# Quarter products for a second gate and up product, from the fourth pair of feature blocks on

## The chip, the core and the metric

The kernel runs on one core of a Trainium2 chip. The core has five engines with a queue each: TensorE (PE; its weight loads are PEld), VectorE (DVE), ScalarE (ACT), GpSimd (POOL) and SyncE (SP, which here only issues DMAs). An engine takes its instructions in the order of its queue and waits at semaphores. The metric is the time of one execution on the device in microseconds, the median of the runs shown.

## What is computed

One layer of an encoder block on 1024 tokens of width 1024, in float32: attention with forget gates and a pooling mixer, an output projection, and a SwiGLU. The change lies in the SwiGLU's first half, the gate and up products with 2816 features each:

```python
h2 = rmsnorm(x, norm2_g[layer])
gate = jnp.einsum('bsd,df->bsf', h2, w_gate[layer])
up = jnp.einsum('bsd,df->bsf', h2, w_up[layer])
x = x + jnp.einsum('bsf,fd->bsd', jax.nn.silu(gate) * up, w_down[layer])
```

## The kernel before

**Precision.** Every operand of a matmul is split into a high half, rounded by ACT, and a low half, the rest, taken by DVE (`split`, L119). A product is three matmuls, high by high, high by low and low by high (`mm3`, L159, so lines L161 to L163 in the profile).

**The stage.** The 22 feature blocks of 128 are taken in eleven pairs (j = 0 to 10). A pair is a 2 x 2 block product in Strassen's form with seven products instead of eight, P1, P2, P6, P7, P5, P3 and P4. The activations are the moving side, as blocks `b11`, `b21`, `t2`, `t3`, `t1`, `b22` and `t4` (high and low, L992) that are made once. The weights are the stationary side: per pair, raw tile 0 holds a11 and a12, raw tile 1 holds a21 and a22 (`gu_raw`, L1040, loaded by SP), and POOL makes four sums s1 to s4 from them (`gu_sums`, L1078): s1 = a21 + a22 for P5, s2 = s1 - a11 for P6, s3 = a11 - a21 for P7, s4 = a12 - s2 for P3. P1 takes a11, P2 a12, P4 a22. The second raw tile of the next pair can be loaded when P4's page has read the present one.

**Pages.** The split weights of one product are a page (`gu_page`, L999): ACT makes its high half, DVE its low half. There are three places for pages, so the page of a product can be made once the product three before it is done. `next_page` (L1358) makes the page two steps ahead, and issues the loads of the raw tiles and POOL's sums for the next pair.

**Products.** `product` (L1020) is 24 matmuls of 512 columns, 12 for the gate bank and 12 for the up bank. P1, P6, P5 and P3 share the banks c1 and go on adding in them; ACT takes a copy in between (`snap`, L1144) as sP1, sU2 and sU4. P2 has the banks c2; P7 and P4 share c3. From pair 1 on, P3 is itself done in Strassen's form, as seven quarter products Q1 to Q7 of six matmuls with 256 columns (`fine_product`, L1249): DVE makes sums of weight quarters in place (`fine_page`, L1224: one sum before page P3a, three before page P3b), and adds each quarter product's bank into the copy sU4. The quarters of P3 are laid among P4's matmuls, in an order written out (L1386). The quarters of the activation block b22 are made once, by `fine_steps` (L1181), during pair 1.

**Results.** The four corners of a pair are made in `after` (L1276): `corner` (L1158) adds a bank and a copy on DVE, takes Silu on ACT and multiplies on POOL. h11 comes from sP1 and P2, h22 from sU4 and P7, h21 from sU2 and P4, h12 from sU4 with P3 in it (Silu on ACT, product on DVE, L1289 and L1290). POOL makes four feature sums f1 to f4 (L1173), and ACT issues the spills of the features to DRAM (`spill`, L1268), from which the down stage reads them later.

**Order.** A pair's steps before are

```python
LATER = ("P1", "P2", "P6", "P7", "P5", "P3a", "P4", "P3b")
```

The order within each engine's queue is found by a planner from dependencies and the order of the program; `tc.issue_after(x)` puts what is issued under it behind x on x's engine.

Of the kernel before, what the change touches and what calls it, by code (L numbers as in the profile page):

```python
# [15 lines left out]
P = 128  # L16
# [29 lines left out]
def tile_kernel(  # L46
# [993 lines left out]
    def gu_raw(j, f, halves=(0, 1)):  # L1040

        if 0 in halves:
            raws[j, f] = xw_tile(f"r{f if j else 1 - f}", f"r{f}_{j}")
        f0 = (2 * j + f) * P
        cs = slice(halves[0] * 4, halves[-1] * 4 + 4)
        for n in range(2):
            dst = raws[j, f][:, n, :].rearrange("p (c e) -> p c e", e=P)
            nc.sync.dma_start(out=dst[:, cs, :], in_=wgu[n][:, cs, f0 : f0 + P])
# [24 lines left out]

    def gu_parts(j):
        r0, r1 = raws[j, 0], raws[j, 1]
        return r0[:, :, 0:512], r0[:, :, 512:1024], r1[:, :, 0:512], r1[:, :, 512:1024]

    def gu_sums(j):  # L1078
        a11, a12, a21, a22 = gu_parts(j)
        s1, s2, s3, s4 = (xw_tile(f"s{i}", f"s{i}_{j}", (P, 2, 512)) for i in (1, 2, 3, 4))  # L1080
        g = nc.gpsimd.tensor_tensor
        g(out=s1, in0=a21, in1=a22, op=ALU.add)  # L1082
        g(out=s2, in0=s1, in1=a11, op=ALU.subtract)
        g(out=s3, in0=a11, in1=a21, op=ALU.subtract)
        g(out=s4, in0=a12, in1=s2, op=ALU.subtract)
# [3 lines left out]
    s1, s2 = ([wk_tile("h", 8, f"s{i}_0{n}") for n in range(2)] for i in (1, 2))  # L1089
# [12 lines left out]
    def sum3():  # L1102
        s3 = operands[0]["P7"] = [wk_tile("h", 8, f"s3_0{n}") for n in range(2)]
# [4 lines left out]
    def sum4(n):  # L1108
        s4 = operands[0].setdefault("P3", [])
        s4.append(wk_tile("h", 8, f"s4_0{n}"))  # L1110
# [33 lines left out]
    def snap(j, key, n):  # L1144
        tag = ("h", 8) if key == "sU4" else ("su" if key == "sU2" else "sp", 2)
        t = snaps[j, key, n] = wk_tile(*tag, f"sn{j}_{key}{n}")
        nc.scalar.activation(out=t, in_=banks["c1", n], func=AF.Copy)
# [4 lines left out]
    def feature(j, name, key):  # L1152
        t = feats[name] = wk_tile("h", 8, f"{name}_{j}")
# [27 lines left out]
    def fine_steps(key):  # L1181
# [5 lines left out]
        t1 = const.tile([P, 2, 2, 256], R, tag="wmask", bufs=1, name=f"fine1_{key}")  # L1187
        fine[key, "Q5"] = t1[:, 0, :, :], t1[:, 1, :, :]

        def small(pl, tag, name):  # L1190
            return pl.tile([P, 2, 256], R, tag=tag, bufs=1, name=f"{name}_{key}")

        fine[key, "Q7"] = small(wk, "e2", "fine3h"), small(xw, "junk2", "fine3l")
        z = {}

        def whole(c, h):
            def do():
                at = ("h", 8) if c else (f"e{h}", 1)
# [10 lines left out]
        def parts(q, at):  # L1209
            def do():  # L1210
                if q == "Q6":
                    fine[key, q] = small(wk, "e0", "fine2h"), small(wk, "e1", "fine2l")
# [10 lines left out]

    def fine_page(j, k, part):  # L1224

        t = operands[j][k]
        p0, p1, p2, p3 = (t[:, n, h] for n in range(2) for h in QTR)

        def go(out, in0, in1, op):
            nc.vector.tensor_tensor(out=out, in0=in0, in1=in1, op=op)  # L1230

        if part == "a":
            go(p2, p0, p2, ALU.subtract)
            hi, lo = gu_page(f"gu{j}_{k}a", t)
            at = dict(Q1=0, Q2=1, Q7=2, Q4=3)
        else:
            go(p2, p3, p2, ALU.subtract)
            go(p1, p1, p2, ALU.subtract)
            go(p0, p0, p2, ALU.add)
# [9 lines left out]
    def fine_product(j, k, q, acc):  # L1249

        at = FINE_BANK[q]
        if q in ("Q1", "Q7", "Q2"):
            fine_banks[at] = bank(f"fine{at}_{j}{k}", *((BANKS["c2", 0], 1) if at == "C" else ("m", 2)))
# [14 lines left out]
    def spill(q=nc.scalar):  # L1268
        while spills:
            d, h = spills.pop(0)  # L1270
# [5 lines left out]
    def after(j, k):  # L1276
        if k in ("P1", "P6", "P5"):
            for n in range(2):
                snap(j, dict(P1="sP1", P6="sU2", P5="sU4")[k], n)
        if k == ("P2" if j else "P5"):  # L1280
            with tc.issue_after(at.ins) if j == 0 else ExitStack():
                corner(j, "h11", "sP1", "c2", "P1")
        if k == h22_from(j):
            corner(j, "h22", "sU4", "c3", "P4")
        if k == "P3":
            corner(j, "h12", None, "c1", None)
        if k == "P3b":
            acc = [snaps[j, "sU4", n] for n in range(2)]
            nc.scalar.activation(out=acc[0], in_=acc[0], func=AF.Silu)  # L1289
            nc.vector.tensor_tensor(out=acc[1], in0=acc[1], in1=acc[0], op=ALU.mult)  # L1290
# [16 lines left out]
    SUMS = dict(P5="b21h", P6="b21l", P7="t2h", P4="t2l")  # L1307
# [299 lines left out]
```

## Time and profile before

| | us |
|---|---|
| median of 3 runs (1032.22 to 1033.70) | 1032.89 |
| the profiled execution | 1032.35 |
| its span, first to last instruction | 1030.5 |
| gate and up stage | 395.60 to 813.60 |
| one pair in it | 37.78 |

The profile's page gives each engine's busy time and the chain of work that ended last, and further views answer single questions: busy time by stretches, the timeline (start, duration, engine, line, what is written from what, and in brackets how long the engine sat idle before it and who ended that), and the DMA issues. Starts are counted from the span's start. Tiles go by the program's names: `gu_P_l` is the low half of a page, `s` a sum of weights, `sn_sU` a copy, `fineA` a bank of quarter products, `r` a raw tile, `h` and `f` features, `hsdP` their place in DRAM.

### The profile page before, as it was taken

To read this page: it belongs to the slowest core of one execution; us is meant where nothing else is said; L and a number is where in the kernel's file an instruction comes from. 1 tells how busy PE (TensorE), PEld (TensorE's weight loads), DVE (VectorE), ACT (ScalarE), POOL (GpSimd) and SP (SyncE) were. 2 spreads that over 40 slices of the span, in tenths; PEclk is the share of its full clock that TensorE was granted. 3 is DMA by queue.
4 is the path that set the end of the run, shared out by engine and by line. 5 is a ranking of instruction groups with operands and counts; after the bars stand their busy time and mean duration, and the time that the engine had idled before them with its cause. 6 is when DMAs were issued, how large, how long until landed. Compare 5 with 4: busy or idle time off the path is not lost.

```text
span 1030.5 us, 14701 instructions
## 1 busy us (share of the span) xinstructions
PE 1021.7 (99%) x5284; PEld 874.5 (85%) x5284; DVE 716.0 (69%) x1132; ACT 464.9 (45%) x747; POOL 405.2 (39%) x315
## 2 busy tenths in 40 slices
PE   9999999999999999999999999999999999999997
PEld 8988888998988888888888888888888888888886
DVE  7565566776886579895556455556547899888886
ACT  7434355665675257533343333433333343333346
POOL 4350121214346043366548548557557410000045
PEclk9999999999999999999999999999999999999999
DMA  7214434333743133333243143233327574452424
GB/s 252 53 47 144 104 81 104 81 99 93 223 177 106 49 133 113 93 113 103 102 143 103 63 142 106 79 123 113 92 103 254 216 256 170 133 183 96 153 92 164
DMA packets 108249, 130.25 MB, mean 126 GB/s; under 512 B 7368, under 2 KB 70352, under 8 KB 108176
## 3 DMA queue, kind: packets, MB, share of 16 engines
q1 hardware_dynamic: 96544, 108.18, 33.2%
q10 hardware_dynamic: 11072, 19.69, 5.0%
q0 software_dynamic: 560, 1.44, 0.4%
q8 instruction: 42, 0.69, 0.3%
q14 instruction: 31, 0.25, 0.1%
HBM read 86.29 MB, written 33.03 MB: 116 GB/s over the span
## 4 chain that ended last, share of the span: by engine, by line
PE 98%; DMA 1%; POOL 0%; DVE 0%; issue 0%; ACT 0%; POOLq 0%; ACTq 0%
PE gu_P L162 12%; PE gu_P L161 12%; PE gu_P L163 12%; PE d L161 6%; PE d L162 6%; PE d L163 6%; PE po L657 4%; PE tp L643 3%; PE o L161 3%; PE qk L161 3%; PE qk L163 3%; PE qk L162 3%; PE o L162 3%; PE o L163 3%; PE v L374 2%; PE z L618 2%
## 5 line engine op out<-in xcount | busy, mean ns | idle before, releaser
L162 PE MATMUL d<-d,d 128*128 128x512 f32 (+1 forms) x308 | 118.6, 388 | 0.0
L163 PE MATMUL d<-d,d 128*128 128x512 f32 (+1 forms) x308 | 118.5, 388 | 0.0
L629 POOL TENSOR_SCALAR p<-p,rr 128x128 f32<-128x128 f32 (+3 forms) x64 | 48.5, 762 | 175.5 <-DVE rr L628 143.9
L161 PE MATMUL d<-d,d 128*128 128x512 f32 x308 | 107.8, 388 | 0.0
L120 ACT ACTIVATE d<-r_f 128x1536 fp32r<-128x1536 f32 (+1 forms) x28 | 38.7, 1384 | 107.6 <-PE d L162 107.6
L1169 POOL TENSOR_TENSOR h<-h,qh 128x512 f32<-128x512 f32 x33 | 64.0, 1941 | 34.5 <-ACT qh L1167 26.7
L1082 POOL TENSOR_TENSOR s<-r 128x1024 f32<-128x1024 f32 x10 | 24.0, 2401 | 131.0 <-DMA r<-in_w_up_dram 84.8
L121 DVE TENSOR_TENSOR gu_P_l<-r,gu_P_h 128x1024 fp32r<-128x1024 f32 x32 | 53.6, 1678 | 29.6 <-ACT gu_P_h L120 29.6
L120 ACT ACTIVATE gu_P_h<-r 128x1024 fp32r<-128x1024 f32 x32 | 33.8, 1059 | 86.2 <-issue 44.2
L1458 POOL TENSOR_SCALAR sse<-sse 128x1 f32<-128x1 f32 x7 | 3.5, 493 | 166.3 <-ACT junk L1454 166.1
L162 PEld LDWEIGHTS d<-d,d 128*128 128x128 f32 x308 | 57.8, 188 | 12.2 <-DVE d L121 0.2
L161 PEld LDWEIGHTS d<-d,d 128*128 128x128 f32 x308 | 57.8, 188 | 12.0
L163 PEld LDWEIGHTS d<-d,d 128*128 128x128 f32 x308 | 57.8, 188 | 11.8
L121 DVE TENSOR_TENSOR gu_P_l<-s,gu_P_h 128x1024 fp32r<-128x1024 f32 (+1 forms) x38 | 52.3, 1384 | 18.2 <-ACT gu_P_h L120 18.1
L626 ACT ACTIVATE p<-p,mn 128x128 f32<-128x128 f32 (+3 forms) x64 | 49.4, 772 | 32.2 <-DVE mn L620 29.3
L648 DVE TENSOR_TENSOR tl<-tp,th 128x512 fp32r<-128x512 f32 (+1 forms) x80 | 49.4, 632 | 9.6 <-ACT th L647 8.6
L121 DVE TENSOR_TENSOR d<-r_f,d 128x1536 fp32r<-128x1536 f32 (+1 forms) x28 | 47.6, 1702 | 6.5 <-ACT d L120 6.5
L163 PE MATMUL qk<-hTh,l_qk 128*128 128x512 f32 x128 | 50.7, 396 | 0.0
L161 PE MATMUL qk<-hTh,h_qk 128*128 128x512 f32 x128 | 50.6, 395 | 0.0
L162 PE MATMUL qk<-hTl,h_qk 128*128 128x512 f32 x128 | 50.4, 394 | 0.0
L647 ACT ACTIVATE th<-tp 128x512 fp32r<-128x512 f32 (+1 forms) x80 | 42.4, 550 | 15.2 <-PE tp L643 12.5
L1562 DVE TENSOR_TENSOR x2f_s<-d,x2f_s 128x512 f32<-128x512 f32 x64 | 42.3, 682 | 10.0 <-PE d L163 9.9
(802 smaller groups left out, 3218.5 us busy)
## 6 DMA issues: line engine op xcount, KB each, us to landing
r_f<-hsdP SPq DMA_DIRECT2D x77, 256.0 KB
r_wd<-in_w_down_dram SPq DMA_DIRECT2D x22, 512.0 KB
r<-in_w_gate_dram SPq DMA_DIRECT2D x21, 512.0 KB
r<-in_w_up_dram SPq DMA_DIRECT2D x21, 512.0 KB
hsdP<-f ACTq DMA_DIRECT2D x40, 256.0 KB
s<-hi SPq DMA_DIRECT2D x64, 128.0 KB
hsdP<-h ACTq DMA_DIRECT2D x32, 256.0 KB
x<-in_x_dram SPq DMA_DIRECT2D x8, 512.0 KB
```

What stands on the lines that cost most here:

```text
L120: mark["hi"] = nc.scalar.activation(out=hi, in_=src, func=AF.Copy)
L121: return eng.tensor_tensor(out=lo, in0=src, in1=f32(hi), op=ALU.subtract)
L161: nc.tensor.matmul(ps, lh, rh, start=start, stop=False, **kw)
L162: nc.tensor.matmul(ps, lh, rl, start=False, stop=False, **kw)
L163: mark["mm"] = nc.tensor.matmul(ps, ll, rh, start=False, stop=stop, **kw)
L626: nc.scalar.activation(out=pr[:, :n], in_=pr[:, :n], func=AF.Exp, scale=-1.0, bias=mn, accum_out=rs)
L629: nc.gpsimd.tensor_scalar(out=pr[:, :n], in0=pr[:, :n], scalar1=rr, scalar2=1.0, op0=ALU.mult, op1=ALU.mult)
L647: nc.scalar.activation(out=th[:, :w], in_=tp[:, :w], func=AF.Copy)
L648: nc.vector.tensor_tensor(out=tl[:, :w], in0=tp[:, :w], in1=f32(th[:, :w]), op=ALU.subtract)
L657: mark["pv"] = nc.tensor.matmul(po[:, first * P : 2 * P], vt[p][:, s, j, :], part[:, o : o + wd], start=(s == 0 and part is th), stop=(s = ...
L1169: nc.gpsimd.tensor_tensor(out=h, in0=h, in1=q, op=ALU.mult)
L1562: added = nc.vector.tensor_tensor(out=row, in0=ps, in1=row, op=ALU.add)
```

## The change

From pair 3 on (`BOTH = 3`), P2 too is done in seven quarter products, laid among P7's matmuls as P3's are among P4's. The block b21 gets quarters of its own, made during pair 2. The steps of such a pair are P1, P6, P2a, P7, P2b, P5, P3a, P4, P3b. The quarters of P2 are added into the copy sP1; h11 is then Silu of one half of it (ACT) times the other (POOL). Several things are put behind others: P7's page behind P2a's; P3a's page behind the addition of P2's last quarter; the three sums for P3b behind P3a's page, and P4's page behind these; POOL's four sums in the order s1 to s4; h12's multiplication behind the page of the next pair's P6. ACT issues the spills of these pairs three steps later. A raw tile is laid out by halves, gate and up next to each other, and loaded in four DMAs instead of two. There are 11 places for the small tiles instead of 8, and the room for them comes from the scratch space of DMA descriptors, set to 2 KB. For the last pair, sums of the down stage go to other tiles (`SUMS`).

```diff
-        for n in range(2):
-            dst = raws[j, f][:, n, :].rearrange("p (c e) -> p c e", e=P)
-            nc.sync.dma_start(out=dst[:, cs, :], in_=wgu[n][:, cs, f0 : f0 + P])
+        for a in halves:
+            to = raws[j, f][:, a, :].rearrange("p (n c e) -> p n c e", n=2, e=P)
+            for n in range(2):
+                nc.sync.dma_start(out=to[:, n, :, :], in_=wgu[n][:, 4 * a : 4 * a + 4, f0 : f0 + P])
...
+    RING = 11
+    BOTH = 3
...
-        g = nc.gpsimd.tensor_tensor
-        g(out=s1, in0=a21, in1=a22, op=ALU.add)
-        g(out=s2, in0=s1, in1=a11, op=ALU.subtract)
-        g(out=s3, in0=a11, in1=a21, op=ALU.subtract)
-        g(out=s4, in0=a12, in1=s2, op=ALU.subtract)
+        at = None
+        for out, in0, in1, op in (
+            (s1, a21, a22, ALU.add), (s2, s1, a11, ALU.subtract), (s3, a11, a21, ALU.subtract), (s4, a12, s2, ALU.subtract)
+        ):
+            with tc.issue_after(at.ins) if at and j >= BOTH else ExitStack():
+                at = nc.gpsimd.tensor_tensor(out=out, in0=in0, in1=in1, op=op)
...
+    def fine_sums(j, k, part):
+
+        p0, p1, p2, p3 = (operands[j][k][:, n, h] for n in range(2) for h in QTR)
+        later = ((p2, p3, p2, ALU.subtract), (p1, p1, p2, ALU.subtract), (p0, p0, p2, ALU.add))
+        for out, in0, in1, op in ((p2, p0, p2, ALU.subtract),) if part == "a" else later:
+            mark["sum"] = nc.vector.tensor_tensor(out=out, in0=in0, in1=in1, op=op)
+        summed.add((j, k, part))
...
         if k in ("P1", "P6", "P5"):
-            for n in range(2):
-                snap(j, dict(P1="sP1", P6="sU2", P5="sU4")[k], n)
-        if k == ("P2" if j else "P5"):
+            with tc.issue_after(mark["P3a"][1].ins) if k == "P5" and j >= BOTH else ExitStack():
+                for n in range(2):
+                    snap(j, dict(P1="sP1", P6="sU2", P5="sU4")[k], n)
+        if k == ("P2" if j else "P5") and j < BOTH:
...
+        if k == "P2b":
+            acc = [snaps[j, "sP1", n] for n in range(2)]
+            with tc.issue_after(mark["hi"].ins):
+                nc.scalar.activation(out=acc[0], in_=acc[0], func=AF.Silu)
+            nc.gpsimd.tensor_tensor(out=acc[1], in0=acc[1], in1=acc[0], op=ALU.mult)
...
-            nc.vector.tensor_tensor(out=acc[1], in0=acc[1], in1=acc[0], op=ALU.mult)
+            with tc.issue_after(mark["page"].ins):
+                nc.vector.tensor_tensor(out=acc[1], in0=acc[1], in1=acc[0], op=ALU.mult)
...
+    LAST = ("P1", "P6", "P2a", "P7", "P2b", "P5", "P3a", "P4", "P3b")
+    todo = [(j, k) for j in range(NG) for k in (LAST if j >= BOTH else LATER if j else FIRST)]
...
+    PIECES = (
+        ("Q1", "Q2", "Q7", (0, (0, 1)), (0, (2, 3)), "Q6", "Q4"), ((1, (0, 1)), "Q5", (1, (2, 3))), ("Q3",),
+    )
+    WINDOWS2 = {"P2a": (0, "P2", "P7"), "P7": (1, "P2", "P7"), "P2b": (2, "P2", "P7")}
+    WINDOWS3 = {"P3a": (0, "P3", "P4"), "P4": (1, "P3", "P4"), "P3b": (2, "P3", "P4")}
...
+        if i + 2 < len(todo) and k != "P2b":
+            with ExitStack() as order:
+                if k in ("P6", "P5") and j >= BOTH:
+                    for ins in (mark["page"], mark["hi"]):
+                        order.enter_context(tc.issue_after(ins.ins))
+                    if k == "P5":
+                        mark["P3a"] = mark["page"], mark["hi"]
+                        fine_sums(j, "P3", "b")
+                        order.enter_context(tc.issue_after(mark["sum"].ins))
+                next_page(*todo[i + 2])
+        waiting.append(spills[:])
+        spills.clear()
+        while len(waiting) > (1 if j < BOTH else 3):
             with tc.issue_after(mark["hi"].ins):
-                spill()
+                spill(waiting.pop(0))
...
+        if k == "P2b":
+            with tc.issue_after(mark["add"].ins):
+                next_page(*todo[i + 2])
...
+        if (j, k) == (BOTH - 1, "P1"):
+            q5, q7 = ([small(wk, f"g{n + m}", f"fine{n}{m}_b21") for m in range(2)] for n in (2, 4))
+            finer += fine_steps("b21", q5, q7, ("g0", "g1"))
...
-    nc = _bacc.Bacc("TRN2", target_bir_lowering=False, num_devices=1)
+    nc = _bacc.Bacc("TRN2", target_bir_lowering=False, num_devices=1, dynamic_dma_scratch_size=2048)
```

More of the change, by code (lines that the diff above doesn't have):

```diff
@@ L1179, in quarter, with small, fine_steps @@
         return t[:, 2 * c : 2 * c + 2, QTR[h]]
-    def fine_steps(key):
+    def small(pl, tag, name):
+        return pl.tile([P, 2, 256], R, tag=tag, bufs=1, name=name)
+    def fine_steps(key, q5, q7, ends):
         bh, bl = blocks[key]
@@ L1222, in fine_steps @@
         ]
+    summed = set()
+    def fine_sums(j, k, part):
[4 more added lines that the diff above has]
+        summed.add((j, k, part))
     def fine_page(j, k, part):
         t = operands[j][k]
-        p0, p1, p2, p3 = (t[:, n, h] for n in range(2) for h in QTR)
-        def go(out, in0, in1, op):
-            nc.vector.tensor_tensor(out=out, in0=in0, in1=in1, op=op)
+        if (j, k, part) not in summed:
+            fine_sums(j, k, part)
         if part == "a":
-            go(p2, p0, p2, ALU.subtract)
             hi, lo = gu_page(f"gu{j}_{k}a", t)
@@ L1266, in fine_product, with spill @@
             mark["add"] = nc.vector.tensor_tensor(out=out, in0=ps, in1=out, op=ALU.add)
-    def spill(q=nc.scalar):
-        while spills:
-            d, h = spills.pop(0)
+    def spill(due, q=nc.scalar):
+        for d, h in due:
             q.dma_start(out=d, in_=h)
```

74 lines of the change are left out of this document (33 added, 41 removed).

## The prediction

> **What bounds the kernel now.** I read the page first: the busy times, then the chain of work that ended last, by engine.
>
> ```profile
> PE 1021.7 (99%) x5284; PEld 874.5 (85%) x5284; DVE 716.0 (69%) x1132; ACT 464.9 (45%) x747; POOL 405.2 (39%) x315
> ...
> PE 98%; DMA 1%; POOL 0%; DVE 0%; issue 0%; ACT 0%; POOLq 0%; ACTq 0%
> ```
>
> TensorE is the chain. The change lies in the gate and up stage, so the next view is busy time by stretches: the whole stage, then one pair of feature blocks in it (pair 4, from the first matmul of its P1 to that of pair 5's).
>
> ```profile
> 395.60:813.60 418.00, 418.00 (x2047) 353.70 (x2046) 265.13 (x321) 163.90 (x223) 240.09 (x116) 1.00 0.35 116
> ...
> 548.36:586.14 37.78, 37.78 (x187) 32.06 (x186) 21.92 (x28) 13.91 (x18) 23.60 (x12) 1.00 0.33 111
> ```
>
> The columns are length, then busy time of PE, weight loads, DVE, ACT and POOL, then the granted clock. TensorE is busy for all 418.00 us at clock 1.00: no wait of another engine reaches the end in this stage. A pair takes 37.78 us, 21.92 of DVE, 23.60 of POOL. So time is won here only by fewer or shorter matmuls, and lost as soon as another engine makes TensorE wait.
>
> **What a product costs.** The timeline of TensorE in pair 4, first matmul of each group: P6 (block t2), P7 (t3), the quarter products Q1 and Q2 of P3, and P1 of the next pair.
>
> ```profile
> 559.99 0.39 PE L161 MATMUL gu_P<-t2h,gu_P_h 128*128 128x512 f32 x1
> ...
> 565.43 0.39 PE L161 MATMUL gu_P<-t3h,gu_P_h 128*128 128x512 f32 x1
> ...
> 576.31 0.28 PE L161 MATMUL fineA_4P<-b22h,gu_P3a_h 128*128 128x256 f32 x1
> ...
> 577.03 0.28 PE L161 MATMUL fineC_4P<-b22h,gu_P3a_h 128*128 128x256 f32 x1
> ...
> 586.14 0.39 PE L161 MATMUL gu_P<-b11h,gu_P_h 128*128 128x512 f32 x1
> ```
>
> The durations overlap; starts count. A whole product is 24 matmuls in 565.43 - 559.99 = 5.44 us, 0.2267 each. A quarter product is 6 matmuls in 577.03 - 576.31 = 0.72 us, 0.12 each. Seven of them are 42 x 0.12 = 5.04. So a product in quarters saves 0.40 us. What switching costs comes from the pair: six whole products and one in quarters are 6 x 5.44 + 5.04 = 37.68, and the pair takes 37.78. The 0.10 left over is the price of going between 256 and 512 columns.
>
> **The change, part by part.** *Removed* in each of the eight pairs 3 to 10: P2 as a whole product (5.44), one page of weights split into a high half (ACT) and a low half (DVE), and the two DVE additions of the corner h11. *Added*: seven quarter products of P2 among P7's matmuls (5.04, and 0.10 for switching, as P3 shows among P4's), two pages, four DVE sums of weight quarters, seven DVE additions. TensorE's sum is 8 x (5.44 - 5.04 - 0.10) = **-2.4 us**. It is the only term on the path as long as the rest is covered; the cover is TensorE's own 37.5 us per pair.
>
> The side engines are priced from the same pair. DVE:
>
> ```profile
> 568.80 1.23 DVE L121 TENSOR_TENSOR gu_P3a_l<-s,gu_P3a_h 128x1024 fp32r<-128x1024 f32 x1 [2.64 <-ACT gu_P3a_h L120]
> 570.06 1.22 DVE L1230 TENSOR_TENSOR s<-s 128x256 f32<-128x256 f32 x3
> 572.00 1.23 DVE L121 TENSOR_TENSOR gu_P_l<-r,gu_P_h 128x1024 fp32r<-128x1024 f32 x1 [0.72 <-ACT gu_P_h L120]
> 574.49 0.69 DVE L1166 TENSOR_TENSOR qh<-gu_P,sn_sU 128x512 f32<-128x512 f32 x1 [1.27 <-ACT sn_sU L1147]
> 577.23 0.42 DVE L1266 TENSOR_TENSOR sn_sU<-fineA_4P,sn_sU 128x256 f32<-128x256 f32 x1 [2.04 <-PE fineA_4P L163]
> 577.57 0.95 DVE L121 TENSOR_TENSOR gu_P3b_l<-s,gu_P3b_h 128x768 fp32r<-128x768 f32 x1
> ...
> 583.87 1.78 DVE L121 TENSOR_TENSOR gu_P_l<-r,gu_P_h 128x1024 fp32r<-128x1024 f32 x1 [0.60 <-ACT gu_P_h L120]
> ...
> 591.29 0.42 DVE L1230 TENSOR_TENSOR s<-s 128x256 f32<-128x256 f32 x1 [2.30 <-POOL s L1085]
> ...
> 594.30 1.78 DVE L1290 TENSOR_TENSOR sn_sU<-sn_sU,sn_sU 128x512 f32<-128x512 f32 x1
> ```
>
> DVE gains a low half of 0.95, four sums (0.42 + 1.22) and seven additions (7 x 0.42), and loses two of 0.69: about +4.2 us, so some 26 of 37.5. As a total it fits. What can fail is order, and the one chain that the new order tightens runs over POOL and a load:
>
> ```profile
> 573.25 0.37 SPq L1048 DMA_DIRECT2D r<-in_w_gate_dram  x1
> ```
>
> ```profile
> 567.71 1.06 ACT L120 ACTIVATE gu_P3a_h<-s 128x1024 fp32r<-128x1024 f32 x1 [1.63 <-POOL h L1169]
> ...
> 589.53 0.60 ACT L1147 ACTIVATE sn_sP<-gu_P 128x512 f32<-128x512 f32 x1 [2.30 <-PE gu_P L163]
> ```
>
> ```profile
> 578.56 2.40 POOL L1082 TENSOR_TENSOR s<-r 128x1024 f32<-128x1024 f32 x1 [11.26 <-DVE gu_P3b_l L121]
> 580.92 2.40 POOL L1084 TENSOR_TENSOR s<-r,r 128x1024 f32<-128x1024 f32 x1
> 583.27 1.29 POOL L1169 TENSOR_TENSOR h<-h,qh 128x512 f32<-128x512 f32 x1
> 584.52 3.39 POOL L1083 TENSOR_TENSOR s<-s,r 128x1024 f32<-128x1024 f32 x1
> 587.99 3.27 POOL L1085 TENSOR_TENSOR s<-r,s 128x1024 f32<-128x1024 f32 x1
> 593.39 2.13 POOL L1169 TENSOR_TENSOR h<-h,qh 128x512 f32<-128x512 f32 x1 [2.13 <-ACT qh L1167]
> ```
>
> These rows show that DVE and POOL exclude each other where both read only SBUF. DVE's low half at 583.87 took 1.78 instead of 1.23: it got going when POOL's 1.29 from 583.27 was over. POOL's sum from 584.52 then took 3.39 instead of 2.40: it had waited for DVE's 1.23. By the page of the Trainium skill "SBUF — State Buffer", section "Who interferes with whom", a DVE instruction with two SBUF inputs and a GpSimd instruction that reads SBUF hold a port pair in turn, for the whole instruction. By that rule, with which these rows agree, added DVE work costs POOL its full length; it speaks against this change, and the port chain among the rivals is what it would do here.
>
> The chain, with T = start of P5. Before, T = 565.43 + 5.44 = 570.87; P4's low half is done at T+2.4, the load of the next pair's second raw tile is issued there (573.25), and POOL's first sum starts 5.3 us later. In the new order P4's page waits behind P3a's page and three sums, and P3a's page waits for the addition of P2's last quarter, which ends at T. An addition starts 0.2 us after its quarter's last matmul slot (577.23 against 577.03). So: addition to T+0.6, first sum to 1.0, P3a's high half (1.06) to 2.1, its low half to 3.3, three sums to 4.6, P4's low half to **T+5.8**; to T+7.1 if POOL's multiplication for h11 (1.29) takes its turn in between. P4 itself needs that half at T + 5.44 + 3 x 0.72 = T+7.6: in time either way. With the 5.3 us of the load, POOL's sums start at T+11.1 to 12.4. They are 4 x 2.40 = 9.6, now back to back, with the low halves of P1 and P6 (2 x 1.23) in turn between them: the fourth ends at T+23.2 to 24.5. P6, now second in order, is due at T+21.4, its low half 0.45 later, so it needs the second sum by about T+19.5 and has it by T+17.1 or 18.4: covered. The quarters of P2 need the fourth sum: one DVE sum (0.42), a high half (1.06), a low half (1.23), 0.1 for hand-overs: **T+26.0 to 27.3**. P2 is due 15.27 us after T (586.14 - 570.87) plus P1, P6 and one quarter product of 0.72: T+26.9, its low half two short matmuls later, **T+27.1**. So this chain, which had several microseconds to spare before, has between +1.1 and -0.2 us. If the multiplications for h12 on DVE (594.30; 0.69 at most without its wait) and for h21 on POOL (593.39; 1.29 without) also come in between, 2.0 us more are gone: -0.9 to -2.2. I take the ends without them, by the nearest row: before, DVE's sum at 591.29 ran the moment POOL's fourth sum was over (587.99 + 3.27), and both multiplications came after it. Then TensorE waits for nothing or 0.2 us, and the term is nothing.
>
> The rest costs nothing, with its cover. The new order puts P6 on the banks right after P1: a copy of 0.60 us by ACT (589.53) must lie between, and each bank has the other's 2.72 us (half of 5.44) for it. The set-up for quarters of b21 in the third pair repeats what the second pair did for b22 inside the stretch in which TensorE never paused. The raw tiles' loads are the same bytes in twice the issues; SP issues four per tile and not two, so at 0.37 us each (the row of 573.25) the last goes out 0.7 us later, while the first pieces move; bounds 0 and 0.7 us in the chain above, of which I take 0. ACT issues the spills three steps later, when their data is there: no wait added. The smaller descriptor space concerns POOL's queue alone:
>
> ```profile
> hsdP<-h POOLq DMA_DIRECT2D x1, 256.0 KB, 4.8
> ```
>
> Even if six such spills at the end of the stage went one by one, that is 6 x 4.8 = 29 us beside 217 us of the down stage (813.60 to 1030.5), whose last group of features alone reads them. Nothing.
>
> **The sum.** The profiled execution took 1032.35 us, its span 1030.5 and 1.85 around it. 1032.35 - 2.4 = 1029.9; the median of the runs shown is 0.54 higher, 1032.89, so the forecast for a median is 1030.5.
>
> **Rivals.** *The port chain is late* (slower). For: POOL's 4 x 2.40 + 7 x 1.29 and DVE's two-input work fill the pair to some 33 of 37.5 us, and the slack worked out above ends at -2.2 us. Against: the order in which the rows show the sum. It decides from the point at which both multiplications go ahead of P2's first sum; price 0.9 to 2.2 us in each of seven pairs (the first pair in the new order still has its sums made in the old one), 6 to 15 us; with the gain, +4 to +13: 1037 to 1046, and more if P2's later pages then fall behind POOL's feature sums too. *Small waits eat the gain* (no change): 0.1 to 0.3 us in each of seven or eight pairs, at P2, or at P4, which has 0.5 us to spare at the late end; 0.7 to 2.4 us given back: 1031.2 to 1032.9. For: the -0.2 above. *Switching costs nothing*: 8 x 0.40 = 3.2: 1029.7. Against: the 0.10 in each of the pairs now.
>
> **Chances.** Forecast 0.45; port chain 0.29; small waits 0.21; free switching 0.05. A measurement of this kernel can tell about 0.2%, 2.1 us, from no change. The forecast is just beyond that, so a tenth of it may read as no change, and the least of the small waits as faster: faster 0.47, same 0.24, slower 0.29. The range of the likeliest alone is 1029.6 to 1031.0. To leave out no more than 2 in 10 it must take in the small waits and the nearer half of the late chain: 1029.4 to 1040.
>
> **What would show it.** Right: in pairs 3 to 10 a stretch of about 37.5 us with TensorE busy throughout, quarter products of P2 at 0.12 us spacing, and DVE's first sum for P2 right behind POOL's fourth sum. Wrong: idle time of TensorE before the first quarter of P2, put down to a page of P2 or to the sum, in pairs 4 to 10 and not in 3; POOL's sums of weights longer than 3 us on average; P4's low half later than 7 us into P5. The prediction fails first at the slack of that chain.

## The result: 12% slower, and the profile after

The changed kernel takes 1152.9 us (median of 5 runs, 1151.2 to 1154.0) against 1032.9: a ratio of 1.116, 95% interval 1.114 to 1.118. The prediction was 1030.5, its range 1029.4 to 1040. The profiled execution took 1151.23 us, its span is 1149.4.

The page of the changed kernel, busy times and the chain that ended last:

```profile
PE 1054.1 (92%) x5428; PEld 895.5 (78%) x5428; DVE 797.8 (69%) x1224; ACT 470.7 (41%) x759; POOL 412.8 (36%) x316
...
PE 33%; DVE 9%; POOL 4%; ACT 3%; DMA 3%; issue 2%; SPq 1%; POOLq 0%; ACTq 0%; DVEq 0%
```

TensorE's share has gone from 99 to 92%, and it is no longer the whole chain. Where the time went shows busy time by stretches, cut at the first matmul of P1. Columns as before: length, then busy time of PE, weight loads, DVE, ACT, POOL, the granted clock. After: the stage, pair 0, pair 2, pair 3, pairs 4 to 9, pair 10.

```profile
395.79:932.34 536.55, 450.48 (x2190) 375.14 (x2189) 346.27 (x413) 169.71 (x234) 247.45 (x117) 0.92 0.28 91
...
395.79:446.99 51.20, 42.61 (x186) 34.71 (x184) 38.61 (x51) 23.98 (x38) 11.17 (x7) 0.90 0.26 78
484.01:528.51 44.50, 40.07 (x188) 33.22 (x186) 36.84 (x40) 15.86 (x23) 29.32 (x13) 0.96 0.29 92
528.51:571.52 43.01, 38.59 (x205) 32.53 (x204) 27.10 (x34) 14.06 (x19) 14.48 (x9) 1.00 0.25 80
```

```profile
571.52:877.31 305.79, 247.54 (x1225) 205.93 (x1224) 179.46 (x217) 85.71 (x114) 144.34 (x67) 0.91 0.24 78
877.31:932.34 55.03, 44.65 (x212) 37.41 (x211) 35.53 (x41) 15.91 (x21) 27.50 (x13) 0.84 0.50 175
```

Before, pair 0 and pair 10:

```profile
395.69:435.67 39.98, 39.98 (x185) 33.12 (x184) 35.59 (x50) 23.67 (x38) 8.24 (x6) 1.00 0.32 100
```

```profile
775.04:813.60 38.56, 38.56 (x194) 32.83 (x193) 28.30 (x29) 15.21 (x20) 22.55 (x11) 1.00 0.63 224
```

The stage is 118.6 us longer, practically the whole growth of the span (118.9). Pair 0 costs 11.2 us, pairs 2 and 3 cost 6.7 and 5.2 (against 37.78), pairs 4 to 9 cost 305.79 - 6 x 37.78 = 79.1, 13.2 each, and pair 10 costs 16.5. The clock, 1.00 throughout before, is down in the stretches with long pauses (0.84 to 0.96), but not in pair 3 (1.00), which has short ones.

What TensorE waited for, in total (what, for whom: us, times, longest):

```profile
PE gu_P L161 <- ACT sn_sP L1150: 50.3, 8, 7.6
PE gu_P L161 <- DVE qh L1169: 12.7, 8, 1.8
PE gu_P L161 <- ACT gu_P_h L120: 8.6, 1, 8.6
```

The first row is the main finding: once in each pair in the new form, the first matmul of P6 waits for ACT's copies sP1 of the banks c1, 6.8 to 7.6 us in pairs 4 to 10 and 1.7 us in pair 3, whose sums of weights POOL had made in the old order, by 523.9 us. The second is P4's first matmul waiting until DVE's additions for h22 have read its bank, the third is in pair 0. The timelines of TensorE, ACT, POOL and DVE around this wait in pair 6:

```profile
679.21 0.39 PE L163 MATMUL gu_P<-b11h,gu_P_l 128*128 128x512 f32 x1
686.45 0.80 PE L161 MATMUL gu_P<-t2h,gu_P_h 128*128 128x512 f32 x1 [6.86 <-ACT sn_sP L1150]
687.05 0.63 PE L162 MATMUL gu_P<-t2l,gu_P_h 128*128 128x512 f32 x1
687.47 0.63 PE L163 MATMUL gu_P<-t2h,gu_P_l 128*128 128x512 f32 x1
```

```profile
683.91 1.06 ACT L120 ACTIVATE gu_P2a_h<-r 128x1024 fp32r<-128x1024 f32 x1 [2.59 <-DVE r L1231]
...
684.88 1.04 ACT L120 ACTIVATE gu_P_h<-s 128x1024 fp32r<-128x1024 f32 x1
685.82 1.06 ACT L1150 ACTIVATE sn_sP<-gu_P 128x512 f32<-128x512 f32 x2
```

```profile
670.48 2.39 POOL L1088 TENSOR_TENSOR s<-r 128x1024 f32<-128x1024 f32 x1 [2.79 <-DMA r<-in_w_up_dram]
...
678.54 3.34 POOL L1088 TENSOR_TENSOR s<-r,s 128x1024 f32<-128x1024 f32 x1
681.84 1.71 POOL L1172 TENSOR_TENSOR h<-h,qh 128x512 f32<-128x512 f32 x1
```

```profile
681.12 1.31 DVE L1303 TENSOR_TENSOR sn_sU<-sn_sU,sn_sU 128x512 f32<-128x512 f32 x1
682.35 1.48 DVE L1231 TENSOR_TENSOR r<-r 128x256 f32<-128x256 f32 x1
```

P1 ends at 679.6. The copies need nothing else, but they are issued at 685.82: on ACT they stand behind the high halves of P2's first page (683.91) and of P7 (684.88). P2's page needs the sum that DVE writes in place into the raw weights (682.35), and that sum needs POOL's fourth sum (678.54 to 681.88), which reads those weights. Two multiplications come in between as well: DVE's for h12 (681.12) starts ahead of the sum, and POOL's for h21 (681.84) runs beside it, so that the sum takes 1.48 instead of 0.42 us. So a copy of 0.6 us hangs on POOL's whole chain of sums by nothing but its place in ACT's queue. After the stop the matmuls are 0.43 us apart (687.05 to 687.47) instead of 0.2267: the wait is paid a second time in the clock.

```profile
686.45:691.50 5.05, 5.05 (x12) 3.98 (x13) 5.01 (x4) 0.44 (x1) 4.55 (x3) 0.50 0.00 0
```

At clock 0.50 for 5.05 us that is another 2.5 us, so 6.9 + 2.5 = 9.4 of a pair's 13.2 us.

Most of the rest begins with P2's last quarter. In pair 5, the first matmul of P5, then that quarter; DVE's addition of it, P3's sum and low half, and P4's low half:

```profile
653.38 0.39 PE L161 MATMUL gu_P<-t1h,gu_P_h 128*128 128x512 f32 x1
...
657.01 0.28 PE L161 MATMUL fineA_5P<-b21h,gu_P2b_h 128*128 128x256 f32 x1
```

```profile
657.92 0.42 DVE L1270 TENSOR_TENSOR sn_sP<-fineA_5P,sn_sP 128x256 f32<-128x256 f32 x1 [5.23 <-PE fineA_5P L163]
658.26 0.42 DVE L1231 TENSOR_TENSOR s<-s 128x256 f32<-128x256 f32 x1
659.88 1.23 DVE L121 TENSOR_TENSOR gu_P3a_l<-s,gu_P3a_h 128x1024 fp32r<-128x1024 f32 x1 [1.21 <-ACT gu_P3a_h L120]
...
663.25 1.22 DVE L121 TENSOR_TENSOR gu_P_l<-r,gu_P_h 128x1024 fp32r<-128x1024 f32 x1
```

The planner had put the quarter 16 matmuls into P5 (16 x 0.2267 = 3.63 us), and P3's page is tied to its addition. P3 and P4 then wait for their pages and banks, in pair 5 some 3.1 us beyond the usual spacing of their matmuls.

### The profile page after: what moved, and what is told of

Same layout as the page of the kernel before. It is cut to its first block, busy times and chain, and to the rows that moved or that the text cites. A ratio compares the mean times of both kernels' runs of the same rounds, so it can differ in the third digit from the quotient of the medians.

```text
span 1149.4 us, 15183 instructions
## 1 busy us (share of the span) xinstructions
PE 1054.1 (92%) x5428; PEld 895.5 (78%) x5428; DVE 797.8 (69%) x1224; ACT 470.7 (41%) x759; POOL 412.8 (36%) x316
## 4 chain that ended last, share of the span: by engine, by line
PE 33%; DVE 9%; POOL 4%; ACT 3%; DMA 3%; issue 2%; SPq 1%; POOLq 0%; ACTq 0%; DVEq 0%
PE d L162 5%; PE d L163 5%; PE d L161 5%; PE gu_P L161 5%; PE gu_P L162 4%; PE gu_P L163 4%; POOL s L1088 3%; DVE gu_P_l L121 2%; DMA r<-in_w_up_dram 2%; DVE s L1231 1%; ACT gu_P_h L120 1%; DVE gu_P3a_l L121 1%; DVE r L1231 1%; DVE sn_sU L1303 1%; SPq L1048 1%
## 5 line engine op out<-in xcount | busy, mean ns | idle before, releaser
L121 DVE TENSOR_TENSOR gu_P_l<-s,gu_P_h 128x1024 fp32r<-128x1024 f32 (+1 forms) x38 | 62.1, 1644 | 41.2 <-ACT gu_P_h L120 41.2
L161 PE MATMUL gu_P<-t2h,gu_P_h 128*128 128x512 f32 x88 | 43.2, 491 | 50.3 <-ACT sn_sP L1150 50.3
L120 ACT ACTIVATE gu_P_h<-s 128x1024 fp32r<-128x1024 f32 (+1 forms) x38 | 36.3, 964 | 97.2 <-POOL s L1088 39.1
L161 PEld LDWEIGHTS gu_P<-t2h,gu_P_h 128*128 128x128 f32 x88 | 21.1, 240 | 58.5 <-ACT sn_sP L1150 53.7
L1296 POOL TENSOR_TENSOR sn_sP<-sn_sP,sn_sP 128x512 f32<-128x512 f32 x8 | 14.9, 1863 | 137.6 <-ACT sn_sP L1295 137.6
L1172 POOL TENSOR_TENSOR h<-h,qh 128x512 f32<-128x512 f32 x25 | 43.4, 1737 | 57.1 <-ACT qh L1170 51.6
L626 ACT ACTIVATE p<-p,mn 128x128 f32<-128x128 f32 (+3 forms) x64 | 49.3, 772 | 31.7 <-DVE mn L620 28.8
L121 DVE TENSOR_TENSOR gu_P_l<-r,gu_P_h 128x1024 fp32r<-128x1024 f32 x24 | 48.3, 2012 | 6.6 <-ACT gu_P_h L120 6.6
```

What stands on the lines that cost most here:

```text
L120: mark["hi"] = nc.scalar.activation(out=hi, in_=src, func=AF.Copy)
L121: return eng.tensor_tensor(out=lo, in0=src, in1=f32(hi), op=ALU.subtract)
L161: nc.tensor.matmul(ps, lh, rh, start=start, stop=False, **kw)
L626: nc.scalar.activation(out=pr[:, :n], in_=pr[:, :n], func=AF.Exp, scale=-1.0, bias=mn, accum_out=rs)
L1172: nc.gpsimd.tensor_tensor(out=h, in0=h, in1=q, op=ALU.mult)
L1296: nc.gpsimd.tensor_tensor(out=acc[1], in0=acc[1], in1=acc[0], op=ALU.mult)
```

## The experiments

Theory A: the copies of P1's banks, late by their place on ACT, are the main cost, and P2's last quarter and pair 0 are costs of their own. Rivals: B, the chain of load, POOL's sums and pages, with the port that DVE and POOL share, sets the pair in any order; C, the ring of 11 small tiles; D, the descriptor space. All ratios are against the kernel before.

| kernel | us | ratio (95%) |
|---|---|---|
| before + 2 KB descriptor space | 1033.4 | 1.000 (0.999 to 1.001) |
| changed, no pair in the new form | 1044.6 | 1.012 (1.010 to 1.013) |
| changed, copies in slots of their own | 1143.2 | 1.106 (1.104 to 1.108) |
| changed, P2's page behind the copies | 1111.1 | 1.076 (1.074 to 1.078) |
| changed, P2's sums in a tile of their own | 1150.8 | 1.115 (1.110 to 1.120) |
| changed, P2's last quarter ahead of P5 | 1120.1 | 1.082 (1.080 to 1.085) |
| changed, set-up of b21 early | 1151.8 | 1.114 (1.113 to 1.116) |
| both orders | 1086.6 | 1.051 (1.049 to 1.054) |
| both orders, first pair's slots, early set-up | 1077.3 | 1.043 (1.041 to 1.045) |
| both orders, features behind P2's page | 1091.8 | 1.056 (1.053 to 1.058) |
| the same, features ahead of P2's page | 1096.7 | 1.062 (1.060 to 1.064) |
| features behind, fourth sum before third | 1098.3 | 1.063 (1.061 to 1.065) |
| the same, first pair's slots, early set-up | 1087.5 | 1.053 (1.050 to 1.055) |
| features behind, without the feature sums | 1064.7 | 1.030 (1.028 to 1.033) |
| features behind, feature sums on DVE | 1073.9 | 1.039 (1.037 to 1.042) |
| the same, first pair's slots, early set-up | 1064.9 | 1.029 (1.026 to 1.032) |

### Descriptor space, and no pair in the new form

```diff
-    nc = _bacc.Bacc("TRN2", target_bir_lowering=False, num_devices=1)
+    nc = _bacc.Bacc("TRN2", target_bir_lowering=False, num_devices=1, dynamic_dma_scratch_size=2048)
```

> The kernel before with the 2 KB descriptor space alone. Theory A (TensorE waits for the copies of the banks that P6 is to add onto, made late by ACT's order): the space takes no part, 1031 to 1035 us. Theory D (the descriptor space slows POOL's queue): over 1040 us.

```diff
-    BOTH = 3
+    BOTH = NG
...
-        if (j, k) == (BOTH - 1, "P1"):
+        if (j, k) == (NG, "P1"):
```

> The changed kernel with no pair in the new form: loading, ring of 11, spills and descriptor space stay changed, P2 is whole and the product order is the old one. Theory A: the first pair keeps its loss of about 11 us, since the copies for P6 stand behind 14 other instructions of ACT there as in the changed kernel, and the other ten pairs take 37.8 us again: 1041 to 1047 us. Rival C (the ring of 11 with its slots, or the loads, cost in every pair): over 1080 us. Rival: the first pair's loss comes from the new form further down: 1031 to 1036 us.

The first shows no change: D falls. The second gives 1044.6, 11.7 us above before, and its later pairs are the old ones; the rows are pair 0 and pair 4:

```profile
396.66:447.67 51.01, 42.40 (x186) 34.62 (x185) 37.97 (x51) 23.98 (x38) 11.05 (x7) 0.90 0.26 78
...
598.03:635.81 37.78, 37.78 (x187) 32.05 (x186) 19.70 (x26) 13.56 (x18) 22.26 (x12) 1.00 0.32 104
```

So the ring, the loads in four DMAs and the descriptor space cost nothing in pairs 1 to 9 of the old form, and 11 us once, in pair 0 (in pair 10 TensorE waits 0.7 us for a page of P3). The spills are issued one step later in this kernel, not three.

### The copies in slots of their own

```diff
-    RING = 11
+    RING = 9
...
-        tag = ("su", 2) if key == "sU2" else ("h", RING)
+        tag = ("h", RING) if key == "sU4" else ("su" if key == "sU2" else "sp", 2)
```

> The changed kernel with the copies of P1's banks back in two slots of their own and a ring of 9 for the rest. Theory A: in the first pair ACT issues these copies in the old place, and its 11 us go; in the later pairs the copies stay behind other work (one of them now behind the spill of the pair before): 1130 to 1150 us. Rival C (sharing the ring is the whole cost): below 1060 us. Rival: the first pair's 11 us have another cause: 1150 us or more, with the first pair still at 51 us.

1143.2 us, 9.7 less. In the changed kernel the copies sP1 had given up two slots of their own and shared the ring; here they have them back. Pairs 0 and 1 together take 77.92 us instead of 88.22. ACT's copies of pair 0 run at 401.0 and 404.0 us (before: 399.4 and 402.3), where the changed kernel has them behind the pages that they used to precede:

```profile
417.72 1.06 ACT L1150 ACTIVATE sn_sP<-gu_P 128x512 f32<-128x512 f32 x2
```

In the changed kernel TensorE's order moved with them: P7, which does not need the copies, went ahead of P6 and waited for its page, and P6 began only at 424.77 (before: 408.48):

```profile
417.32 0.79 PE L161 MATMUL gu_P<-t3h,gu_P_h 128*128 128x512 f32 x1 [8.59 <-ACT gu_P_h L120]
```

That wait and the slow matmuls behind it (PE busy 42.6 instead of 40.0 us in pair 0) are the 11 us. Giving the copies a place in the ring let the planner move them; in pairs 5 to 9 own slots don't help (259.0 us, against 255.3). C is right for pair 0 alone.

### P2's page behind the copies

```diff
-        if i + 2 < len(todo) and k != "P2b":
+        if i + 2 < len(todo) and k != "P2b" and not (k == "P1" and j >= BOTH):
...
+        if k == "P1" and j >= BOTH:
+            with tc.issue_after(mark["snap"].ins):
+                next_page(*todo[i + 2])
```

> The changed kernel with one order changed: in pairs 3 to 10 P2's first page is issued on ACT behind the two copies of the banks and no longer ahead of them. Theory A: the stop of 7.0 us in P1 and 2.4 us in P6 goes in pairs 4 to 10; P2's first page is then late for its first quarter by 0.5 to 2 us; 7 x 7.4 to 8.9 = 52 to 62 us less: 1091 to 1101 us. Rival B (the chain over POOL's sums sets the pair in any order, the copies only stand where it shows): the wait goes to P2's first quarter in full: 1145 to 1153 us.

1111.1 us: 41.8 less, where 52 to 62 were expected. The order was a cause, rival B (1145 or more) is out, but the copies were not free yet. ACT, in pair 5:

```profile
622.59 0.63 ACT L1301 ACTIVATE sn_sU<-sn_sU 128x512 f32<-128x512 f32 x1 [2.79 <-DVE sn_sU L1270]
623.19 0.63 ACT L1170 ACTIVATE qh<-qh 128x512 f32<-128x512 f32 x1
623.73 1.07 ACT L1150 ACTIVATE sn_sP<-gu_P 128x512 f32<-128x512 f32 x2
```

Now they stand behind the two Silus for h12 and h21 of the pair before, which wait for DVE.

### P2's sums in a tile of their own

```diff
-    RING = 11
+    RING = 9
...
-        later = ((p2, p3, p2, ALU.subtract), (p1, p1, p2, ALU.subtract), (p0, p0, p2, ALU.add))
...
+        later = ((y2, p3, y3, ALU.subtract), (y1, p1, y2, ALU.subtract), (y0, p0, y2, ALU.add))
...
```

> The changed kernel with the sums of P2's quarters in a tile of their own, not in place of the raw weights, so that P2's pages no longer wait until POOL's fourth sum has read them; the ring has 9 slots to make room. Theory A (the copies stand behind P2's page, and that behind the fourth sum): the copies come 4 to 6 us earlier in seven pairs, behind the third sum: 1111 to 1125 us. Rival C (slots of the ring, whose spills must have landed, hold the copies): no better than the changed kernel, 1148 us or more.

1150.8 us, the rival's figure. P2's first page is now made early (681.01 in pair 6), but the copies are still late:

```profile
688.14 0.60 ACT L1153 ACTIVATE sn_sP<-gu_P 128x512 f32<-128x512 f32 x1 [2.53 <-DVE sn_sU L1317]
```

They stand behind P7's page, and their wait is put down to DVE's multiplication for h12, which presumably still reads the slot that they are to have, in a ring cut to 9. With two things changed at once, this run doesn't speak about the fourth sum.

### P2's last quarter ahead of P5, alone and with the other order

```diff
-            for n in range(2):
-                product(j, k, n)
+            with tc.issue_after(mark["mm"].ins) if k == "P5" and j >= BOTH else ExitStack():
+                for n in range(2):
+                    product(j, k, n)
```

> The changed kernel with P2's last quarter put ahead of P5 in pairs 3 to 10 (it stood 16 matmuls into P5). Theory A with two separate parts: the waits of 1.1, 0.4 and 2.1 us in P3 and P4, which come of P3's first page standing behind that quarter's addition, go in eight pairs, 29 us; the stop for the copies in P1 and P6 moves with P1 and stays at 9.4 us: 1118 to 1130 us. Rival: the quarter has to wait for the addition before it on the same bank, TensorE stops there, and nothing is won: 1148 to 1165 us.

> Both orders at once: P2's last quarter ahead of P5, and P2's first page behind the copies of P1's banks on ACT. If the two costs are separate, the 29 us come off the 1111 us of the second alone: 1075 to 1092 us. If the chain over the load and POOL's sums sets the pair however it is ordered (rival B): 1105 us or more.

1120.1 and 1086.6 us, both as theory A had it: 32.8 us less alone, 24.5 less on top of the other order. The costs are separate for the most part (41.8 + 32.8 = 74.6, together 66.4). A pair is down to 41.7 us at clock 1.00, here pair 6:

```profile
650.05:691.71 41.66, 38.53 (x206) 32.52 (x204) 30.18 (x37) 14.19 (x19) 22.52 (x12) 1.00 0.29 95
```

### The set-up of b21's quarters

```diff
-        for _ in range(min(3 if j == 1 and k in ("P1", "P2") else 2, len(finer))):
+        for _ in range(min(3 if j in (1, 2) and k in ("P1", "P2") else 2, len(finer))):
```

> The changed kernel with the set-up of b21's quarters in pair 2 issued three steps a product at first, as b22's is in pair 1, so that it ends ahead of P3. Theory (the loss of some 6.4 us in P3 and P4 of pair 2 is this set-up taking turns with POOL's sums of weights at the port): 1145 to 1149 us. Rival (pair 2 loses by the new order of the pair behind it): 1151 to 1155 us.

1151.8 us: 1.1 less, a miss. The loss of pair 2 itself was rightly read. In the changed kernel its set-up takes turns with POOL's sums of weights, 2.27 us for a sum that takes 0.68 alone, and the additions of quarters that free P3's banks stand behind it:

```profile
516.62 2.27 DVE L1200 TENSOR_TENSOR fine_b<-b21h,b21l 128x512 f32<-128x512 f32 x1
518.81 0.41 DVE L1270 TENSOR_TENSOR sn_sU<-fineC_2P,sn_sU 128x256 f32<-128x256 f32 x1
```

With the set-up early, pair 2 takes 39.2 us instead of 44.5. But the time only moved: pair 3 takes 49.3 us instead of 43.0. In it TensorE waits 2.90 us, and its matmuls are slow behind that, because the low half of P1's own page stands on DVE behind P2's first sum, which waits 5.23 us for POOL's fourth sum.

```profile
525.22 0.42 DVE L1231 TENSOR_TENSOR r<-r 128x256 f32<-128x256 f32 x1 [5.23 <-POOL s L1088]
525.56 1.22 DVE L121 TENSOR_TENSOR gu_P_l<-r,gu_P_h 128x1024 fp32r<-128x1024 f32 x1
```

### What is left: the features and the port

With both orders, pairs 4 to 9 still take 41.6 to 42.4 us. The next kernel puts the features h12 and h21 behind the copies and P2's page; the one after that also has the fourth sum before the third.

```diff
+        elif k == "P3b" and j >= BOTH:
+            held = j, k
...
             with tc.issue_after(mark["snap"].ins):
                 next_page(*todo[i + 2])
+                if j > BOTH:
+                    after(*held)
```

> The kernel with both orders (P2's last quarter ahead of P5, P2's first page behind the copies), and the features h12 and h21 of the pair before, with their two functions on ACT, also behind the copies. Theory: the rest of the stop in P1 and P6 (2.4 to 3.2 and up to 1.7 us a pair) is these two standing ahead of the copies while their additions wait on DVE behind the low half of P6, which takes turns with POOL's sums; with them behind, about 2 us remain at P2's first quarter, which hangs on the fourth sum: 7 x 2 to 3 = 14 to 21 us less than 1086.6: 1064 to 1075 us. Rival (the chain over the load and the sums sets the pair, and P2's page is late by as much as the copies were): 1082 us or more.

```diff
-            (s1, a21, a22, ALU.add), (s2, s1, a11, ALU.subtract), (s3, a11, a21, ALU.subtract), (s4, a12, s2, ALU.subtract)
+            (s1, a21, a22, ALU.add), (s2, s1, a11, ALU.subtract), (s4, a12, s2, ALU.subtract), (s3, a11, a21, ALU.subtract)
```

> The same, and POOL's fourth sum ahead of its third in pairs 3 to 10. Theory (what is left in these pairs is P2's first page behind the fourth sum): that page comes 2.4 to 3.3 us earlier and TensorE no longer waits for it, 7 x 1.5 to 2 = 10 to 14 us less than the kernel without it. Rival (P7's page, which needs the third sum, is then late in its place): within 4 us of the kernel without it.

```diff
+                if j > BOTH:
+                    after(*held)
                 next_page(*todo[i + 2])
-                if j > BOTH:
-                    after(*held)
```

> The kernel with both orders and the features behind the copies but ahead of P2's first page on ACT. Theory (the features lost by being moved behind that page, where they fall among P2's and P7's pages): between the two places of before, 1074 to 1086 us. Rival (the time is set by the port whatever their place): 1086 us or more.

1091.8, 1098.3 and 1096.7 us: none faster than both orders alone, and all three expectations missed, the first and the third at their rivals' figures. With the features behind P2's page the stop for the copies is all but gone, and waits of 3.1 us stand at P7: 1.43 us for its low half, then 1.20 and 0.51 us for P2's second page. DVE, between P2's pages, with the features behind P2's page:

```profile
667.99 2.30 DVE L121 TENSOR_TENSOR gu_P_l<-s,gu_P_h 128x1024 fp32r<-128x1024 f32 x1
670.21 2.94 DVE L1231 TENSOR_TENSOR r<-r 128x256 f32<-128x256 f32 x2
```

P7's low half takes 2.30 instead of 1.22 us and two sums 2.94 instead of 0.75: POOL's feature sums are running, and one of them, from 669.28, takes 2.15 us where the one before it took 1.40. POOL's queue itself isn't late: it is through with these sums at 674.3, sits idle for 10.6 us, and its next sums of weights wait for their load (2.28 us, at 695.05). To tell the port from the chain, POOL's side was taken away, by leaving the four sums out, and by giving them to DVE:

```diff
-        t = feature(j, name, key)
-        nc.gpsimd.tensor_tensor(out=t, in0=feats[a], in1=feats[b], op=op)
+        if j < BOTH:
+            t = feature(j, name, key)
+            nc.gpsimd.tensor_tensor(out=t, in0=feats[a], in1=feats[b], op=op)
+        else:
+            feats[name] = feats[a]
+            spills.append((hsd[key, j], feats[a]))
```

> The kernel with both orders and the features behind the copies, without POOL's four feature sums in pairs 3 to 10 (left out of the computation; the features that they would read are written to DRAM in their place, as many bytes). Theory: what is left there is the port; the four sums and the sums and low halves of DVE take turns between P2's and P7's pages, so without them DVE's low half for P7 takes 1.2 and not 2.3 us, the three sums for P2's second page 0.4 and not 1.5 each, and the 3.1 and 0.7 us at P7 and behind it go for the most part: 7 x 3 to 4.5 = 21 to 32 us less than 1091.8: 1060 to 1071 us. Rival (what is left is the chain of the load, POOL's sums of weights and the pages): 1085 us or more.

```diff
-        nc.gpsimd.tensor_tensor(out=t, in0=feats[a], in1=feats[b], op=op)
+        eng = nc.vector if BOTH <= j < NG - 1 else nc.gpsimd
+        eng.tensor_tensor(out=t, in0=feats[a], in1=feats[b], op=op)
...
+        if k == "P7" and j > BOTH:
+            with tc.issue_after(mark["page"].ins):
+                feature_sums(j - 1)
```

> The kernel with both orders and the features behind the copies, with the four feature sums of pairs 3 to 9 on DVE, behind its low half for P5, and not on POOL. All is computed. Theory (the port, not the work, was the price): DVE has the room, P7's low half and P2's sums stay short, and the time comes near the one without the sums, 1064.7 us, with at most 0.8 us a pair more: 1063 to 1073 us. Rival (DVE's own work is then the bound): 1080 us or more.

1064.7 and 1073.9 us, 27.1 and 18.0 less. The first kernel also takes four tiles a pair fewer from the ring; the second takes as many as before, so places in the ring don't explain its gain. The same DVE instructions without the sums, and then the pairs, without the sums and with them on DVE:

```profile
659.88 1.22 DVE L121 TENSOR_TENSOR gu_P_l<-s,gu_P_h 128x1024 fp32r<-128x1024 f32 x1
661.01 0.75 DVE L1235 TENSOR_TENSOR r<-r 128x256 f32<-128x256 f32 x2
```

```profile
646.36:684.53 38.17, 37.84 (x205) 32.52 (x204) 26.34 (x37) 14.11 (x19) 15.52 (x8) 1.00 0.32 104
```

```profile
645.81:685.56 39.75, 38.49 (x206) 32.59 (x204) 26.83 (x40) 14.40 (x19) 15.57 (x8) 1.00 0.32 100
```

More instructions on DVE made the pair shorter than the same sums on POOL had, 39.75 us against 41.6 to 43.9: the port was the price, not the work. The sums changed their place too, from among P2's and P7's pages to behind P5's low half; POOL doing them in that place was not tried. The time is just above the expected range. TensorE waits 0.6 us for P2's first low half and 0.3 us at P4; three of the sums, 0.6 us apart, go ahead of the addition of P2's last quarter, on which P3's page and, behind it, P4's hang, but what that order costs was not tested.

### All together

```diff
+        if (j, key) == (0, "sP1"):
+            tag = f"g{n + 2}", 1
...
-        for _ in range(min(3 if j == 1 and k in ("P1", "P2") else 2, len(finer))):
+        for _ in range(min(3 if j in (1, 2) and k in ("P1", "P2") else 2, len(finer))):
```

These two edits were put on three of the kernels above.

> The same, and the two copies of the first pair in slots of their own, and the set-up of b21 three steps a product. Theory (the losses of the pairs are separate and add): the first pair's 11 us go, and of pairs 2 and 3 some 5 us: 14 to 17 us less than the kernel without these two edits. With it the sum of what is left stands: above 1033 us as long as any pair in the new form waits for more than the 0.3 us that it saves.

> The kernel with both orders, P2's last quarter ahead of P5 and P2's first page behind the copies, and besides the first pair's copies in slots of their own and the set-up of b21 three steps a product. Theory (the four costs are separate and add): 1086.6 less 11 for the first pair and 3 to 6 for pairs 2 and 3: 1069 to 1073 us. Rival (a saving of one turns up as a wait in another): 1076 us or more.

> The same, and the first pair's copies in slots of their own and b21's set-up three steps a product. Theory: 9 to 14 us less than the kernel without these two: 1049 to 1062 us; still above the kernel before, as the pairs in the new form stay near 38.5 us against 37.8. Rival: within 6 us of the kernel without them.

1087.5, 1077.3 and 1064.9 us: 10.8, 9.2 and 9.0 us less than without the two, and all above what was expected. The savings don't add. With both orders, pairs 0 and 1 together take 80.5 us instead of 87.7, so 7.1 of the first pair's 11 us come back; TensorE now waits 2.3 us at P7 of pair 1. The early set-up wins 5.1 us in pair 2 and loses 3.2 in pair 3, as above. The last kernel is the fastest that computes everything, and still 2.9% slower than the kernel before. No pair in the new form came below 39.2 us in it: of the 32 us that are left, some 18 lie in pairs 3 to 9 (282.1 us against 7 x 37.78) and 9 in pair 10. What pair 10 loses was not tested by a run of its own; in the changed kernel its trace shows the same stop for the copies (6.86 us) and waits of 2.0 and 1.4 us for P3's first page.

## Why the prediction was wrong, step by step

- **TensorE's own sum, -2.4 us**: the price of a quarter product holds; those of P2 are 0.71 us apart (first matmuls of Q1 and Q2 in pair 5, below). The pair of 37.5 us was seen in no run. The shortest in the new form, pair 9 without the feature sums, took 37.94 us, with one gap of some 0.3 us in it:

```profile
643.56 0.28 PE L161 MATMUL fineA_5P<-b21h,gu_P2a_h 128*128 128x256 f32 x1
...
644.27 0.28 PE L161 MATMUL fineC_5P<-b21h,gu_P2a_h 128*128 128x256 f32 x1
```

- **The copy between P1 and P6, "each bank has the other's 2.72 us"**: this is the step that failed. It priced the copy by its length and its inputs, as if ACT were idle. Before it in ACT's queue stood P2's first page, which is tied to POOL's fourth sum, and P7's page, and before these two Silus, which are tied to DVE. Cost: 6.9 us of waiting and 2.5 us of clock a pair in pairs 4 to 10. Moving P2's page alone gave back 41.8 us.
- **P4's low half at T+5.8 to 7.1**: it came at 663.25 + 1.22 - 653.38 = T+11.1, the sign named beforehand ("later than 7 us into P5"). The step assumed that P2's last quarter ends at T; it was put 16 matmuls into P5. With the quarter where the prediction had it, the rest of the chain was sized well. In the kernel with both orders, T = 634.75, P4's low half and P2's first sum and low half on DVE, and POOL's fourth sum:

```profile
640.30 1.22 DVE L121 TENSOR_TENSOR gu_P_l<-r,gu_P_h 128x1024 fp32r<-128x1024 f32 x1
...
658.71 1.50 DVE L1231 TENSOR_TENSOR r<-r 128x256 f32<-128x256 f32 x1 [0.72 <-POOL s L1088]
660.14 0.68 DVE L1303 TENSOR_TENSOR sn_sU<-sn_sU,sn_sU 128x512 f32<-128x512 f32 x1
661.34 1.94 DVE L121 TENSOR_TENSOR gu_P2a_l<-r,gu_P2a_h 128x1024 fp32r<-128x1024 f32 x1 [0.53 <-ACT gu_P2a_h L120]
```

```profile
655.34 3.33 POOL L1088 TENSOR_TENSOR s<-r,s 128x1024 f32<-128x1024 f32 x1
```

  P4's low half is done at T+6.8 (5.8 to 7.1 predicted). POOL's sums start at T+12.5 (11.1 to 12.4): the load took 5.7 us from its first issue and not 5.3, the last of its four issues going out 1.1 us after the second, where 0.7 was the bound and nothing was taken. The fourth sum is done at T+23.9 (23.2 to 24.5), P2's page at T+28.5. That is 1.2 us past the end that was taken (26.0 to 27.3) and 1.4 past its due time of T+27.1: POOL's multiplication for h21 went ahead of the sum (1.50 instead of 0.42 us) and a feature sum ahead of the low half (1.94 instead of 1.23). Of the first rival's condition that is one half, at a cost inside its price. In the changed kernel itself the condition was met in full, as the rows of pair 6 show (681.12 and 681.84): the forecast had taken the order of the nearest row, in which both multiplications came after the sum.
- **The rival of the port** was right in kind and too small. It priced 0.9 to 2.2 us a pair, at P2's first page. The larger price, which it named without a figure ("more if P2's later pages then fall behind POOL's feature sums too"), lies between P2's two pages, where POOL's feature sums and DVE's sums and low halves take turns: 27.1 us over the seven pairs from 4 on, 3.9 each. The rule that the prediction draws on (the Trainium skill, "SBUF — State Buffer", "Who interferes with whom") is borne out by the pair of fences above, 2.30 against 1.22 us for one instruction.
- **The set-up of b21 at nothing**, because pair 1 did the like without a pause: wrong by 6.7 us in pair 2. In pair 1 it was over at 471.8 us and POOL's sums began at 476.8; in pair 2 it ran until 524.4, and they began at 512.9.
- **The ring of 11** was not priced at all, as a change of space only. That the copies sP1 gave up their own slots for it cost 11 us in pair 0.
- **The descriptor space, the loads in four DMAs, the later spills at nothing**: the first is confirmed by itself, the loads in so far as pairs of the old form with them take the old 37.78 us. No run has the spills three steps later on their own, so that term stays open.

## What to carry to other kernels

An instruction that was given nothing to wait for still waits for all that stands ahead of it on its engine; before pricing a short copy at nothing, list what the engine's queue holds in front of it and what the last of these hangs on. Where an order is found by a planner, a new slot, an in-place write or a tie can move an instruction by microseconds, so a step's place has to be read from the queue and not from the program. A gain of 0.3 us a pair isn't worth a schedule in which three engines must all be on time.

## What the runs showed of the hardware

A wait of TensorE can cost more than its length. In the changed kernel each of the seven stops of 6.8 to 7.6 us was followed by a granted clock of 0.50; in pair 6 that lasted 5.05 us, 2.5 us more. A shorter one did it too: in the kernel with both orders, a stop of 2.27 us was followed by clock 0.68, one of 2.97 us in the next pair by 1.00. The length of the stop alone doesn't decide it.

```profile
574.65:580.00 5.35, 5.35 (x16) 4.24 (x17) 4.77 (x4) 3.05 (x4) 4.31 (x4) 0.68 0.01 3
616.99:622.00 5.01, 4.99 (x22) 4.12 (x23) 4.41 (x4) 2.95 (x4) 3.96 (x4) 1.00 0.00 0
```

The Trainium skill's page "TensorE: Matmul & The Clock Gate" puts the rule, in the section "HAM oscillation — how this bites in real kernels", at no idle gaps of more than about 3.4 us. The runs agree in that every stop of 6.8 us or more was followed by half the clock, and they show a slow stretch behind a shorter gap of 2.27 us as well.
